# Expert gate and up columns in two slices of 1792 instead of four, with six PSUM banks taken in turn

## The chip, the cores and the metric

The kernel runs on one core of a Trainium2 chip. The metric is the time of one execution on the device in microseconds (us); the rows and the profile come from one execution taken by the hardware profiler, the other times from runs of the same program without it.

## What is computed

A two-layer encoder trunk on 256 tokens of 1024 features, all in float32: an attention mixer and a dense feed-forward in layer 0, an attention mixer and a mixture of experts in layer 1. The change touches the experts alone. There are eight, each with 3584 hidden columns, and each token goes to the two that its router ranks first:

```python
def swiglu(x, w_gate, w_up, w_down):
    return (jax.nn.silu(x @ w_gate) * (x @ w_up)) @ w_down
...
    for e in range(N_EXPERTS):
        y = y + combine[:, e:e + 1] * swiglu(xt, w_gate[e], w_up[e], w_down[e])
```

The kernel computes an expert only for the tokens sent to it, but it must read all three weight matrices: 3 x 1024 x 3584 x 4 bytes = 44.04 MB an expert, 352 MB for eight.

## The kernel before, in words

**Tokens in slots.** For a pair of experts, `gather` (L848) multiplies the tokens by a selection matrix, so that `gx` holds 128 token slots for each expert, features on the partitions. An expert uses 64 or 96 of them, in sets of 32: two sets for the three experts with few tokens ("narrow": the third, fifth and eighth to be computed), three for the other five ("wide"; `WIDE`). A set of 32 slots fills 32 columns of the TensorE array, so each matmul is written as four side by side (`q` in `gate_up`), each with a quarter of the weight columns; their outputs stand on four groups of 32 partitions.

**Slices.** `SLICES` (L886) cuts the 3584 columns into 1024, 1024, 768 and 768. For each slice `gate_up` (L914) runs through the gate matrix and then the up matrix. `load_raw` (L195) brings two chunks of 128 rows in one DMA: on each partition two runs of 4 KB (3 KB for the narrow slices), so four DMAs for each matrix and slice. For each chunk, set and `q` there is one matmul of 256 (192) columns (L929), recorded in the trace as two, with a weight load for each. Sets 0 and 1 of a matrix share a PSUM bank and the third sets of gate and up share another, so a slice takes two banks, or three if wide, from `mm_bank` (four, by turns). ACT then takes Silu of gate (L933, L938), DVE multiplies by up (L934, L939), and `h_turn` (L943) transposes the result on DVE in blocks of 32 into `hT`, which has two buffers. `down` (L957) multiplies `hT` by the slice's rows of the down matrix, 256 rows (1 MB, one run of 8 KB on each partition) a DMA, and adds all slices of an expert up in the banks a0 and a1.

**Order on TensorE.** The loop from L1068 issues the down product one slice late: gate and up of slice j, then the down product of slice j-1 (`late`), with the gather for the next pair between its steps at an odd expert's last slice. In slice 1 the previous expert's output is scattered: `scatter` (L990), once before `late` and once after it, two banks a2 and a3 each time, evicted by DVE (L1001); then `expert_start` (L900) transposes this expert's selection matrix in one bank. At the very end the last slice's down product follows the one before it directly, and then come the last scatter, the layer norm and the stores.

**Order on the DMA queue.** All weights are loaded by SP's queue in the order of their use. `raw_tile` (L152) takes the buffer from `rooms` (L1037), a fixed round of 20 buffers of 1 MB in various pools:

```python
    rooms += ([(extra[0], "xraw", {})] * 7 + [(wp, "raw", {})] * 4 + [(wp, "hi4", {"bufs": 1}), (wp, "lo4", {"bufs": 1})]
              + [(wp, "hi", {"bufs": 3}), (wp, "lo", {"bufs": 3})] * 3 + [(xp, "xTl", {})])
```

So a load starts when TensorE is done with the load 20 places before it, and SP waits at its head for that. The first 20 are issued while layer 1's mixer and router still run.

**Small tiles.** `pack` (L893, the slot numbers that `expert_start` compares with) lies in the buffer "gb" that the layer norms' scales used before; the experts' output `y` (L984) and `ST`, `hb`, `hT` lie in the pool `ep`.

Of the kernel before, what the change touches and what calls it, by code (L numbers as in the profile page):

```python
# [65 lines left out]
def tile_encoder(ctx: ExitStack, tc: tile.TileContext, x_in, emb_g, emb_b, w_in, b_gate, na_rpb, sw_sink,  # L66
# [13 lines left out]
    def mm_bank():  # L80
        return pp.tile([128, 512], F32, tag="mm", name="mm")
# [13 lines left out]
    def tr_bank():  # L95
        flip[0] ^= 1
        return acc_bank(2 + flip[0])
# [747 lines left out]
        dve.tensor_scalar(cmi, cmax, float(SLOTS), None, op0=OP.add)  # L845
        return res[0], res[1], who, cap, cmi

    def gather(S_sel, n, bank=lambda c2: mm_bank()):  # L848

        gx = xp.tile([128, KC, 256], F32, tag="xTh", name="gx")[:, :, :n]  # L850

        pss = {}

        def token_tile(c2, t):

            if not t:
                pss[c2] = bank(c2).rearrange("p (c s) -> p c s", c=2)[:, :, :n]
            for i in range(2):
                c = 2 * c2 + i
                for k, src in enumerate((xth, xtl)):  # L860
                    pe.matmul(pss[c2][:, i], src[:, t, c * 128:(c + 1) * 128], S_sel[:, t], start=i + k + t == 0,
                              stop=i + k + t == 3)

        def out(c2):
            g, b = ln_col(3, 2 * c2)
            act.activation(gx[:, 2 * c2], pss[c2][:, 0], AF.Identity, bias=b, scale=g)
            g, b = ln_col(3, 2 * c2 + 1)
            dve.tensor_scalar(gx[:, 2 * c2 + 1], pss[c2][:, 1], g, b, op0=OP.mult, op1=OP.add)

        def step(c2):  # L870
            for t in range(2):
                token_tile(c2, t)
            out(c2)

        return gx, [lambda c2=c2: step(c2) for c2 in range(KC // 2)], (token_tile, out)
# [7 lines left out]

    SLICES = [(0, 1024), (1024, 1024), (2048, 768), (2816, 768)]  # L886
    LASTJ = len(SLICES) - 1

    pack = {}

    def new_pack():

        pk = xp.tile([128, 256], F32, tag="gb", name="pack", bufs=1)  # L893
        pool.tensor_copy(pk[:, 0:128].rearrange("p (a s) -> p a s", a=2),
                         iota[:, None, 0:SA].to_broadcast([128, 2, SA]))
        pool.tensor_copy(pk[:, 128:256].rearrange("p (a s) -> p a s", a=4),
                         iota[:, None, SA:SLOTS].to_broadcast([128, 4, SB]))
        pack["rows"] = pk

    def expert_start(pcols, wide=True):  # L900

        S2 = part_tile([128, 2, 256], "S2")
        na = 1 + wide
        for t in range(2):
            dve.tensor_scalar(S2[:, t, 0:128 * na], pack["rows"][:, 0:128 * na], pcols(t), None, op0=OP.is_equal)
        ps = tr_bank().rearrange("p (a s) -> p a s", a=2)
        for a in range(na):
            for t in range(2):
                pe.transpose(ps[:, a, t * 128:(t + 1) * 128], S2[:, t, a * 128:(a + 1) * 128], ident)
        ST = ep.tile([128, 2, S], F32, name="ST")  # L910
        dve.tensor_copy(ST[:, 0:na], ps[:, 0:na])
        return ST

    def gate_up(wg, wu, gx, j, wide=True):  # L914

        c0, W = SLICES[j]
        nk, Q = 2048 // W, W // 4
        A, B = [], mm_bank() if wide else None
        for b, w in enumerate((wg, wu)):
            A.append(mm_bank())  # L920
            sets = [A[b][:, 0:Q], A[b][:, Q:2 * Q]] + ([B[:, b * 256:b * 256 + Q]] if wide else [])
            for kk in range(KC // nk):
                wt = load_raw(w[:, kk * nk:(kk + 1) * nk, c0:c0 + W], nk, W)
                for k in range(nk):
                    c = kk * nk + k
                    for s, out in enumerate(sets):

                        for q in range(4):
                            pe.matmul(out[q * 32:q * 32 + 32], gx[:, c, s * 32:s * 32 + 32],  # L929
                                      wt[:, k, q * Q:(q + 1) * Q], start=c == 0 and s != 1, stop=c == KC - 1 and s != 0)  # L930
        n = 3 if wide else 2
        h = part_tile([128, 512], "eh")[:, 0:2 * Q]
        act.activation(h, A[0][:, 0:2 * Q], AF.Silu)  # L933
        dve.tensor_mul(h, h, A[1][:, 0:2 * Q])  # L934
        parts = [(h, 2)]
        if wide:
            hb = ep.tile([128, 256], F32, name="hb")[:, 0:Q]
            act.activation(hb, B[:, 0:Q], AF.Silu)  # L938
            dve.tensor_mul(hb, hb, B[:, 256:256 + Q])  # L939
            parts.append((hb, 1))  # L940
        return parts

    def h_turn(parts):  # L943

        hT = ep.tile([128, 768], F32, name="hT", bufs=2)
        out = []
        at = 0
        for v, n in parts:
            N = v.shape[1]
            nb = N // n // 32  # L950
            dve.transpose(hT[:, at:at + N], v.rearrange("p (s f b) -> p s b f", s=n, f=32))
            out += [hT[:, at + i * 32 * nb:at + (i + 1) * 32 * nb].rearrange("p (b s) -> p b s", b=nb)
                    for i in range(n)]
            at += N
        return out

    def down(wd, hT, yb, j, between=(), final=False):  # L957

# [22 lines left out]
            step()  # L981

    def expert_out(yb):
        y = ep.tile([128, 2, 512], F32, name="y")  # L984
        act.activation(y[:, 0], yb[0], AF.Copy)
        if len(yb) > 1:
            dve.tensor_copy(y[:, 1], yb[1])
        return y[:, 0:len(yb)]

    def scatter(ST, y, ccols, t, bank=tr_bank):  # L990

        tk = slice(t * 128, (t + 1) * 128)
        pss = [bank() for _ in range(2)]
        k = y.shape[1]
        for a in range(k):
            for n in range(2):
                r = slice(n * 64, n * 64 + 64)
                pe.matmul(pss[n], ST[r, a, tk], y[r, a], start=a == 0, stop=a == k - 1)
        for n in range(2):
            ns = slice(n * 512, (n + 1) * 512)  # L1000
            dve.scalar_tensor_tensor(xt[:, t, ns], pss[n], ccols(t), xt[:, t, ns], op0=OP.mult, op1=OP.add)  # L1001
# [66 lines left out]
    for e in range(NE):  # L1068
        Sp, gx, _ = pair
        hs = slice(e % 2 * 128, e % 2 * 128 + 128)  # L1070
        wide = WIDE[e]
        if e < FIXED:
            wg, wu, wd = mgv[:, e], muv[:, e], moe_d[0, e:e + 1]
        else:
            it = nc.values_load(turns[2][0:1, e - FIXED:e - FIXED + 1], engines=[SP], min_val=0, max_val=NE - 1,
                                skip_runtime_bounds_check_because="a sum with one term, the index of an expert")
            wg, wu = (w[:, ds(it, 1)].rearrange("p e c n -> p (e c) n") for w in (mgv, muv))
            wd = moe_d[0, ds(it, 1)]
        for j in range(LASTJ + 1):
            final = e == NE - 1 and j == LASTJ  # L1080
            with ExitStack() as es:
                if e == j == 0:
                    es.enter_context(tc.manual_schedule(engines={PE}))
                h = gate_up(wg, wu, gx[:, :, hs], j, wide)
            hT = h_turn(h)
            if e == 0 and j == 1:
                comb = route_weights()
                turns += take_turns(comb)
            steps = []
            if j == LASTJ and e % 2 and e + 1 < NE:  # L1090
                pair = pair_start(e // 2 + 1)
                steps = pair[2]
            if j == 1 and ends:
                ends.pop(0)()
            if final:
                act.activation(sd[:, 0:1], eps, AF.Sqrt)
            if late:
                late(steps)
            if j == 1 and ends:
                ends.pop(0)()  # L1100
            if j == 1:
                ST = expert_start(lambda t: turns[0][:, t, e:e + 1], wide)
            if j == 0:
                yb = [acc_bank(n) for n in range(1 + wide)]

            def late(between, e=e, j=j, hT=hT, wd=wd, ST=ST if j else None, yb=yb, final=final):
                ccols = lambda t: turns[1][:, t, e:e + 1]
                down(wd, hT, yb, j, between, final)
                if j == LASTJ:
                    y = expert_out(yb)  # L1110
                    if not final:
                        ends.extend(lambda t=t: scatter(ST, y, ccols, t) for t in range(2))
                        return
                    for t in range(2):
                        scatter(ST, y, ccols, t, mm_bank)
                        out_part(t)
                        out_stats(t)

# [90 lines left out]
```

## Time and profile before

| | |
|---|---|
| runs | 1467.33, 1468.05, 1471.76 us (median 1468.05) |
| the profiled execution | 1467.57 us; its span on the core 1465.4 us |
| mean granted TensorE clock | 0.983 of 2.4 GHz |
| busy, share of the span | PE matmuls 95%, PE weight loads 71%, DVE 36%, ACT 23%, POOL 9% |
| instructions | 37823, of them 17251 matmuls and as many weight loads |
| DMA | 451.93 MB, 442.91 MB of it by SP's queue |

A matmul counts as busy from its start to a modelled end, and several run at a time, so a busy PE need not be at its limit. The DMA share is the busy time of the 16 DMA engines' packets; it can exceed 1, since packets of one engine overlap a little. Times in rows are microseconds from the start of the span. The experts' stage lasts from 595 us to the end.

### The profile page before, as it was taken

What the parts mean: (1) busy time and instruction counts of PE and PEld (TensorE: products, weight loads), DVE (VectorE), ACT (ScalarE), POOL (GpSimd) and SP (SyncE); (2) the same over time, 40 slices, a digit from 0 to 9 for tenths busy, and PEclk for the clock granted to TensorE, in tenths of its full rate; (3) what the DMA queues carried; (4) which work ended last, traced back from release to release, by engine and by line L of the source; (5) the groups of instructions that cost most, each with busy time, mean ns of one, the idle gap of its engine ahead of it and who ended that gap; (6) DMA issues with size and microseconds to landing.
All of it is one profiled execution on the core that took longest, in us unless ns stands there. A gap on an engine that the chain in (4) does not pass through costs nothing. (4 is left out here: it accounts for less than half of the span.)

```text
span 1465.4 us, 37823 instructions
## 1 busy us (share of the span) xinstructions
PE 1392.5 (95%) x17251; PEld 1033.5 (71%) x17251; DVE 521.5 (36%) x707; ACT 338.0 (23%) x543; POOL 125.6 (9%) x71
## 2 busy tenths in 40 slices
PE   7999989999899998899999999999979999999974
PEld 5989989999788896557967558766444475459741
DVE  8675685455687656501110210111201101210203
ACT  4566444444356752100000100001000000000000
POOL 5210050000360100400000000000000000000000
PEclk8999999999999999999999999999999999999998
DMA  8833546555483498699999999999999999999993
GB/s 293 236 126 128 173 132 230 184 173 173 144 238 118 123 395 302 211 343 411 408 335 403 409 407 410 408 408 410 408 408 411 396 404 410 401 400 411 399 409 148
DMA packets 155668, 451.93 MB, mean 308 GB/s; under 512 B 8032, under 2 KB 57568, under 8 KB 141296
## 3 DMA queue, kind: packets, MB, share of 16 engines
q1 hardware_dynamic: 153536, 442.91, 80.1%
q0 software_dynamic: 1968, 6.55, 1.5%
q8 instruction: 137, 2.24, 0.6%
q14 instruction: 27, 0.22, 0.0%
HBM read 448.38 MB, written 1.05 MB: 307 GB/s over the span
## 5 line engine op out<-in xcount | busy, mean ns | idle before, releaser
L929 PE MATMUL mm<-raw,gx 128*32 128x192 f32 (+1 forms) x10752 | 528.0, 353 | 15.9 <-DMA raw<-in_moe_w_up_dram 7.2
L929 PEld LDWEIGHTS mm<-raw,gx 128*32 128x32 f32 x10752 | 395.7, 110 | 149.7 <-issue 21.3
L971 PE MATMUL a<-raw,hT 128*32 128x512 f32 x1792 | 223.1, 600 | 14.4 <-DMA raw<-in_moe_w_down_dram 9.6
L934 DVE TENSOR_TENSOR eh<-eh,mm 128x512 f32<-128x512 f32 (+1 forms) x32 | 19.9, 621 | 583.6 <-PE mm L929 583.6
L192 DVE TENSOR_TENSOR lo<-raw,hi 128x2048 fp32r<-128x2048 f32 x78 | 191.6, 2464 | 89.9 <-ACT hi L185 89.7
L203 PE MATMUL mm<-xTh,hi 128*128 128x256 f32 x704 | 202.3, 287 | 0.0
L205 PE MATMUL mm<-xTh,lo 128*128 128x256 f32 x704 | 200.0, 284 | 0.0
L204 PE MATMUL mm<-xTl,hi 128*128 128x256 f32 x704 | 199.7, 284 | 0.0
L185 ACT ACTIVATE hi<-raw 128x2048 fp32r<-128x2048 f32 (+1 forms) x85 | 158.7, 1873 | 74.2 <-PE mm L204 43.2
L971 PEld LDWEIGHTS a<-raw,hT 128*32 128x32 f32 x1792 | 80.1, 111 | 120.3 <-issue 79.8
L203 PEld LDWEIGHTS mm<-xTh,hi 128*128 128x128 f32 x704 | 134.6, 191 | 7.2 <-issue 5.4
L205 PEld LDWEIGHTS mm<-xTh,lo 128*128 128x128 f32 x704 | 134.6, 191 | 3.1 <-issue 3.1
L204 PEld LDWEIGHTS mm<-xTl,hi 128*128 128x128 f32 x704 | 134.7, 191 | 1.8 <-issue 1.5
L933 ACT ACTIVATE eh<-mm 128x512 f32<-128x512 f32 (+1 forms) x32 | 17.4, 544 | 510.1 <-PE mm L929 510.1
L976 PE MATMUL a<-raw,hT 128*32 128x512 f32 x560 | 82.7, 592 | 0.0
L1124 POOL DMA_DIRECT2D raw<-in_ln_g_dram x1 | 0.6, 616 | 794.2 <-DMA raw<-in_moe_w_down_dram 794.2
L205 PE MATMUL mm<-hi,xTl 128*128 128x256 f32 (+1 forms) x128 | 46.6, 365 | 6.9 <-DVE xTl L273 6.9
L976 PEld LDWEIGHTS a<-raw,hT 128*32 128x32 f32 x560 | 28.7, 110 | 31.5 <-issue 27.8
L938 ACT ACTIVATE hb<-mm 128x256 f32<-128x256 f32 (+1 forms) x20 | 7.2, 358 | 186.0 <-PE mm L929 186.0
L203 PE MATMUL mm<-hi,xTh 128*128 128x256 f32 (+1 forms) x128 | 46.4, 367 | 3.8 <-DVE xTh L272 3.8
L204 PE MATMUL mm<-lo,xTh 128*128 128x256 f32 (+1 forms) x128 | 46.0, 361 | 0.2 <-DVE lo L192 0.2
L192 POOL TENSOR_TENSOR lo<-raw,hi 128x1024 fp32r<-128x1024 f32 (+1 forms) x7 | 23.9, 3416 | 249.4 <-ACT hi L185 249.4
(237 smaller groups left out, 1378.9 us busy)
## 6 DMA issues: line engine op xcount, KB each, us to landing
raw<-in_moe_w_down_dram SPq DMA_DIRECT2D x111, 1024.0 KB, 17.1
raw<-in_moe_w_gate_dram SPq DMA_DIRECT2D x64, 1024.0 KB, 18.6
raw<-in_moe_w_up_dram SPq DMA_DIRECT2D x64, 1024.0 KB, 18.3
raw<-in_moe_w_gate_dram SPq DMA_DIRECT2D x64, 768.0 KB, 17.7
raw<-in_moe_w_up_dram SPq DMA_DIRECT2D x64, 768.0 KB, 14.8
raw<-in_w_in_dram SPq DMA_DIRECT2D x32, 1024.0 KB, 6.2
raw<-in_ffn_w_gate_dram SPq DMA_DIRECT2D x11, 1024.0 KB, 5.5
raw<-in_ffn_w_up_dram SPq DMA_DIRECT2D x11, 1024.0 KB, 5.4
```

The lines of the kernel that those rows point to most:

```text
L185: act.activation(hi[:, p], raw[:, p], AF.Copy)
L192: eng.tensor_sub(lo[:, p], raw[:, p], hi[:, p])
L203: pe.matmul(o, lh, rh, start=first, stop=False)
L204: pe.matmul(o, lh, rl, start=False, stop=False)
L205: pe.matmul(o, ll, rh, start=False, stop=last)
L929: pe.matmul(out[q * 32:q * 32 + 32], gx[:, c, s * 32:s * 32 + 32], wt[:, k, q * Q:(q + 1) * Q], start=c == 0 and s != 1, stop=c == KC - 1 ...
L933: act.activation(h, A[0][:, 0:2 * Q], AF.Silu)
L934: dve.tensor_mul(h, h, A[1][:, 0:2 * Q])
L938: act.activation(hb, B[:, 0:Q], AF.Silu)
L971: pe.matmul(yb[0][r:r + 32], hT[s][:, m], w[:, n * 512:(n + 1) * 512], start=first, stop=last)
L976: pe.matmul(yb[1][r:r + 32], hT[2][:, m - 1 + i], wt[:, i, n * 512:(n + 1) * 512], start=j == 0 and m == 1, stop=last)
L1124: pool.dma_start(gf, ln2_g[1].partition_broadcast(128))
```

## The change

The columns are cut into two slices of 1792, one chunk of 128 rows a DMA (one run of 7 KB on each partition), eight DMAs for each matrix and slice; a buffer of 1 MB then holds 0.875 MB. A matmul has 448 columns. Each set of a matrix has a bank of its own, so a wide slice takes six and a narrow one four. All of them, and those of `scatter`, `gather` and `expert_start`, come from `late_bank`, which goes round the four `mm` banks and a2 and a3. `h` has one tile for all sets, in `ep`; `hT` has one buffer, so `h_turn` is moved behind `late`, and in the last slice it gets a buffer out of the weights' round instead. `pack` moves into `ep`, and `y` into "gb". With two slices the scatters, `expert_start` and the gather for the next pair all belong to slice 1.

```diff
-    SLICES = [(0, 1024), (1024, 1024), (2048, 768), (2816, 768)]
+    SLICES = [(0, FE // 2), (FE // 2, FE // 2)]
...
+    def late_bank():
+
+        spin[0] = (spin[0] + 1) % 6
+        return acc_bank(spin[0]) if spin[0] in (2, 3) else mm_bank()
...
-        pk = xp.tile([128, 256], F32, tag="gb", name="pack", bufs=1)
+        pk = ep.tile([128, 256], F32, name="pack")
...
-        ps = tr_bank().rearrange("p (a s) -> p a s", a=2)
+        ps = late_bank().rearrange("p (a s) -> p a s", a=2)
...
     def gate_up(wg, wu, gx, j, wide=True):
...
+        Q = W // 4
+        ns = 3 if wide else 2
+        banks = []
+        for w in (wg, wu):
+            outs = [late_bank()[:, 0:Q] for _ in range(ns)]
+            banks.append(outs)
+            for c in range(KC):
+                wt = load_raw(w[:, c:c + 1, c0:c0 + W], 1, W)[:, 0]
+                for s, out in enumerate(outs):
+                    for q in range(4):
+                        pe.matmul(out[q * 32:q * 32 + 32], gx[:, c, s * 32:s * 32 + 32], wt[:, q * Q:(q + 1) * Q],
+                                  start=c == 0, stop=c == KC - 1)
+        h = ep.tile([128, 3, FE // 8], F32, name="h")
+        for s in range(ns):
+            act.activation(h[:, s, 0:Q], banks[0][s], AF.Silu)
+            dve.tensor_mul(h[:, s, 0:Q], h[:, s, 0:Q], banks[1][s])
+        return h[:, 0:ns, 0:Q]
+
+    def h_turn(h, room=None):
+
+        ns, Q = h.shape[1:]
+        hT = (ep.tile([128, 3 * FE // 8], F32, name="hT") if room is None else room)[:, 0:ns * Q]
+        dve.transpose(hT, h.rearrange("p s (f b) -> p s b f", f=32))
+        return [hT[:, s * Q:(s + 1) * Q].rearrange("p (b s) -> p b s", s=32) for s in range(ns)]
...
     def expert_out(yb):
-        y = ep.tile([128, 2, 512], F32, name="y")
+        y = xp.tile([128, 2, 512], F32, tag="gb", name="y", bufs=1)
...
-        pss = [bank() for _ in range(2)]
+        pss = [late_bank() for _ in range(2)]
...
                 h = gate_up(wg, wu, gx[:, :, hs], j, wide)
-            hT = h_turn(h)
...
             if j == 0:
                 yb = [acc_bank(n) for n in range(1 + wide)]

+            hT = h_turn(h, raw_tile() if final else None)
+
             def late(between, e=e, j=j, hT=hT, wd=wd, ST=ST if j else None, yb=yb, final=final):
```

## Rows read from the trace of the kernel before

**Rows 1.** The page: GB/s in 40 equal slices of the span; costliest group of instructions

```profile
GB/s 293 236 126 128 173 132 230 184 173 173 144 238 118 123 395 302 211 343 411 408 335 403 409 407 410 408 408 410 408 408 411 396 404 410 401 400 411 399 409 148
...
L929 PE MATMUL mm<-raw,gx 128*32 128x192 f32 (+1 forms) x10752 | 528.0, 353 | 15.9 <-DMA raw<-in_moe_w_up_dram 7.2
```

**Rows 2.** Two stretches: length, busy time (count) by engine, clock, DMA share, GB/s

```profile
core 0: us, PE busy (x) PEld busy (x) DVE busy (x) ACT busy (x) POOL busy (x), PEclk, DMA share, GB/s
...
776.00:1395.00 619.00, 604.50 (x9716) 383.38 (x9717) 84.25 (x142) 27.90 (x55) 0.00 (x0) 0.99 1.02 407
...
598.00:776.00 178.00, 176.71 (x3021) 123.45 (x3009) 29.17 (x56) 6.66 (x14) 8.58 (x6) 1.00 0.97 362
```

**Rows 3.** SP's waits, 602 to 776 us: us in total, times, longest

```profile
SPq L199 <- PE mm L929: 100.3, 52, 4.5
```

**Rows 4.** SP's waits, 776 to 1395 us

```profile
SPq L199 <- DMA raw<-in_moe_w_up_dram: 113.4, 77, 2.2
```

**Rows 5.** PE's waits, 776 to 1446 us: us in total, times, longest

```profile
PE a L971 <- DMA raw<-in_moe_w_down_dram: 9.6, 10, 1.9
PE mm L929 <- DMA raw<-in_moe_w_up_dram: 7.2, 13, 2.0
PE a L971 <- SPq L1130: 4.8, 5, 2.6
...
PE mm L929 <- DMA raw<-in_moe_w_gate_dram: 3.2, 7, 0.7
```

**Rows 6.** Timeline of PE: start, length, what, count [idle before, and what ended it]

```profile
1074.79 1.92 PE L971 MATMUL a<-raw,hT 128*32 128x512 f32 x16 [1.00 <-DMA raw<-in_moe_w_down_dram]
...
1082.27 1.92 PE L971 MATMUL a<-raw,hT 128*32 128x512 f32 x16 [0.56 <-DMA raw<-in_moe_w_down_dram]
...
1086.19 1.51 PE L929 MATMUL mm<-raw,gx 128*32 128x192 f32 x32 [0.37 <-DMA raw<-in_moe_w_gate_dram]
...
1095.95 1.51 PE L929 MATMUL mm<-raw,gx 128*32 128x192 f32 x32 [0.46 <-DMA raw<-in_moe_w_up_dram]
1099.46 1.58 PE L929 MATMUL mm<-raw,gx 128*32 128x192 f32 x32 [2.00 <-DMA raw<-in_moe_w_up_dram]
...
1403.36 1.92 PE L971 MATMUL a<-raw,hT 128*32 128x512 f32 x16 [1.00 <-DMA raw<-in_moe_w_down_dram]
...
1443.05 3.64 PE L971 MATMUL a<-raw,hT 128*32 128x512 f32 x32 [0.47 <-SPq L1130]
```

**Rows 7.** DMA packets, 840 to 852 us; by queue: packets, MB, share of 16 engines

```profile
DMA packets 1525, 4.86 MB, mean 405 GB/s; under 512 B 90, under 2 KB 90, under 8 KB 1441
...
q1 hardware_dynamic: 1523, 4.82, 102.5%
```

**Rows 8.** DMA packets, 808 to 825 us

```profile
DMA packets 1765, 6.95 MB, mean 409 GB/s; under 512 B 107, under 2 KB 107, under 8 KB 1729
...
q1 hardware_dynamic: 1764, 6.93, 102.2%
```

**Rows 9.** DMA packets, 855 to 862 us

```profile
DMA packets 517, 2.86 MB, mean 408 GB/s; under 512 B 47, under 2 KB 47, under 8 KB 243
...
q1 hardware_dynamic: 516, 2.84, 99.4%
```

**Rows 10.** The instruction queue's packets, 776 to 1395 us

```profile
q8 instruction: 76, 1.25, 0.8%
```

**Rows 11.** The instruction queue's packets, 1075 to 1403 us

```profile
q8 instruction: 39, 0.64, 0.8%
```

**Rows 12.** GB/s in 40 equal slices of 511 to 598 us

```profile
GB/s 148 412 418 416 407 411 411 405 396 392 409 392 422 392 392 360 405 185 0 23 296 348 380 367 405 162 282 409 301 397 412 443 422 347 79 4 0 72 177 0
```

**Rows 13.** Line 929 alone in two stretches: length, PE and PEld busy (count), clock, DMA

```profile
597.00:635.00 38.00, 38.00 (x712) 21.13 (x708) 1.00 0.89 310
1319.00:1334.00 15.00, 14.56 (x361) 13.73 (x356) 1.00 1.02 409
```

**Rows 14.** Groups by shape, 600 to 1465 us: count, busy us, mean ns, idle before

```profile
L951 DVE STREAM_TRANSPOSE hT<-eh 128x512 f32<-128x512 f32 x16 | 17.9, 1122 | 0.6
...
L934 DVE TENSOR_TENSOR eh<-eh,mm 128x512 f32<-128x512 f32 x16 | 11.0, 688 | 287.6 <-PE mm L929 287.6
```

More of the change, by code (lines that the diff above doesn't have):

```diff
@@ L846, in take_turns, with gather @@
         return res[0], res[1], who, cap, cmi
-    def gather(S_sel, n, bank=lambda c2: mm_bank()):
+    def gather(S_sel, n, bank=lambda c2: late_bank()):
         gx = xp.tile([128, KC, 256], F32, tag="xTh", name="gx")[:, :, :n]
@@ L880, in select @@
             dve.tensor_scalar(S_sel[:, t, sl], iota, pcols(t), None, op0=OP.is_equal)
-    SLICES = [(0, 1024), (1024, 1024), (2048, 768), (2816, 768)]
+    SLICES = [(0, FE // 2), (FE // 2, FE // 2)]
     LASTJ = len(SLICES) - 1
     pack = {}
+    spin = [0]
+    def late_bank():
+        spin[0] = (spin[0] + 1) % 6
+        return acc_bank(spin[0]) if spin[0] in (2, 3) else mm_bank()
     def new_pack():
-        pk = xp.tile([128, 256], F32, tag="gb", name="pack", bufs=1)
+        pk = ep.tile([128, 256], F32, name="pack")
         pool.tensor_copy(pk[:, 0:128].rearrange("p (a s) -> p a s", a=2),
@@ L916, in gate_up @@
         c0, W = SLICES[j]
[L917 to L955, printed above, removed]
+        Q = W // 4
@@ L988, in expert_out, with scatter @@
         return y[:, 0:len(yb)]
-    def scatter(ST, y, ccols, t, bank=tr_bank):
+    def scatter(ST, y, ccols, t):
         tk = slice(t * 128, (t + 1) * 128)
-        pss = [bank() for _ in range(2)]
+        pss = [late_bank() for _ in range(2)]
         k = y.shape[1]
@@ L1114, in late @@
                     for t in range(2):
-                        scatter(ST, y, ccols, t, mm_bank)
+                        scatter(ST, y, ccols, t)
                         out_part(t)
```

## The prediction

> **What bounds the kernel now.** The page's GB/s by slices comes first [rows 1]: from the 19th slice on, about 660 us, the core moves some 400 GB/s with one dip, and it does so to the end. That is the experts' stage, which must read 352 MB. The windows then tell two parts of it apart [rows 2]: 362 GB/s at a DMA share of 0.97 from 598 to 776 us, and 407 GB/s at 1.02 from 776 to 1395 us. PE is busy throughout in both, but that count is no proof, so the waits decide.
>
> In the first part SP waits for TensorE alone, 52 times for matmuls of line 929 [rows 3]: the 20 buffers are full, and a load starts when a matmul gives one back. Two wide experts are computed there, and PE sets the pace. In the second part SP waits for landed loads too [rows 4], and PE stands waiting for loads, 9.6 + 7.2 + 4.8 + 3.2 = 24.8 us in all [rows 5]. (The 4.8 us are put down to SP's line 1130, but they lie in the last down product, whose steps come at the pitch of its loads; I count them as loads.) The timeline shows that pace: matmuls start 1.95 us apart on loads of 768 KB and 2.49 us apart on those of 1 MB [rows 6]. Wide experts put PE behind, narrow ones let it catch up, and the DMA engines never rest. So from 776 us to the last down steps, which run from 1443.05 to 1446.7 us, the DMA engines set the end; what follows, 18.7 us of a span of 1465.4, is untouched by the change.
>
> **The price of a run.** Three windows hold packets of mostly one size. In [rows 7] 90 packets are tiny, 1351 are of 3 KB and 82 of 8 KB; in [rows 8] 1622 are of 4 KB and 35 of 8 KB; in [rows 9] 196 are of 3 KB and 273 of 8 KB. Share x 16 engines x length gives 196.8, 278.0 and 111.3 us of packet time, from which follow 126.5 ns for 3 KB, 164.6 for 4 KB and 317 for 8 KB. A straight line through the latter two has 12 ns that do not depend on the size, and puts 7 KB at 278.9 ns. Shares above 1 mean that packets overlap a little, so these 12 ns are an upper bound.
>
> The pace of landing gives the net price. Each engine takes 16 packets of a 768 KB load: 5 loads from 1086.19 to 1095.95 us [rows 6], 1.952 us each, 122.0 ns a packet. A down load is 8 packets of 8 KB: 7.48 us for three, 2.493 each, 311.6 ns a packet. Their line has a fixed part of 8.2 ns and gives 159.9 ns for 4 KB (a 1 MB load of gate or up: 2.558 us) and 273.7 ns for 7 KB (a new load of 8 packets an engine: 2.189 us).
>
> **The change, part by part.**
>
> *Longer runs.* Two old loads take 2.558 + 1.952 us, two new ones 2 x 2.189: 0.066 us saved for each of 32 loads an expert. The number of loads stays 46 an expert, as do the bytes. The saving counts where DMA sets the pace, for the last six experts: 192 x 0.066 = **12.6 us**. No row has a packet of 7 KB. Upper bound, by the packets' own times: 8 x 12.2 ns x 192 = 18.7 us (25 us if all eight experts count). Lower bound, at 3 KB's rate by the byte: 1.952 x 7/6 = 2.277 us, a loss of 4 us. At 4 KB's rate by the byte, 2.238 us, 3 us are saved. I take the line, since packets on both sides of 7 KB lie on it.
>
> There is a rule against this. The Trainium skill, "DMA: Bandwidth & Descriptors", section "Bandwidth", puts the fixed overhead at about 3 cycles a packet beside one cycle for 32 bytes, and calls joining descriptors worth it only up to 256 bytes. By that page two runs of 3 and 4 KB become one for 227 instead of 230 cycles, an estimate of 1.3%, 5.6 us of the 433 us that those 192 loads take, and the sum below would end at 1455.3 us. The trace does not agree: its rows have more than twice that price a packet.
>
> *Fewer instructions to load.* Half as many matmuls for gate and up, each twice as wide on average. Wide experts have 1536 recorded matmuls there and narrow ones 1024 (5 and 3 of them make the 10752 of [rows 1]); three of each follow 776 us, so 3840 matmuls and 3840 weight loads go. The instruction queue fetched 76 packets of 16 KB while PE ran 9716 + 9717 instructions [rows 2, 10], 256 for each; 30 packets go. One packet takes 0.8% x 16 x 619 / 76 = 1.04 us on its engine, which delays everyone's landing somewhat: in [rows 6] one load comes 3.51 us after the one before it instead of 1.95. From 1074.79 to 1403.36 us lie exactly three experts' loads; at the pace above they need 3 x (16 x 2.558 + 16 x 1.952 + 14 x 2.493) = 321.2 us and took 328.6, with 39 such packets [rows 11]: 0.19 us each. **5.7 us** saved; if they spread evenly over the engines, 30 x 1.04 / 16 = 2 us.
>
> *The first two experts.* PE sets their pace. A matmul of 256 columns comes every 38/712 = 53.4 ns, one of 192 every 41.6 [rows 13]. At 256's rate by the column one of 448 takes 93.5 ns, and 24 of them 2.24 us a wide load; before, 48 took (2.56 + 2.00) / 2 = 2.28. Over 64 loads that saves 2.6 us, and by the line through both sizes 10 us; some evictions are added, so I take **1 us**, between nothing and 10. The 20 buffers, full from about 586 us while PE is not ready [rows 12], hold some 2.5 MB less then, 6 us of transfer. I take nothing: PE's release of buffers paces the loads from there to 776 us, its lead is 20 loads either way, and a load averages 44.04/46 MB before and after.
>
> *Banks and evictions.* As many elements are evicted, by DVE and ACT that are mostly idle. Six banks in one fixed round let the next gate phase start on banks that the last Silu freed half a slice ago, and scatter, gather and the selection's transposes take the following ones. Cover: gate's or up's eight loads, at least 12 us, beside three products of at most 0.69 us [rows 14]. If the cover is gone, see the second rival.
>
> *One hT, turned later.* The transposes of a slice now wait for the down product before it, and the next Silu, behind them on DVE's order, for them. 1344 columns at 1122/512 ns are 2.9 us [rows 14], while PE runs a gate phase. In the last slice, where no gate phase follows, the round's buffer lets them run beside seven loads of down, 17 us. Taken as nothing; uncovered, 16 x 2.9 = 47 us.
>
> *The rest.* SP issues as many loads in the same order and gets no new wait; the last hT takes one buffer of 20 for 14 loads while only 7 or so are under way. `pack` and `y` change places with neither read sooner than before. The gather's four steps move from among three down loads to among seven, so their evictions end earlier relative to the next gate phase. Nothing for each, an estimate of 1 us either way together.
>
> **Sum.** 12.6 + 5.7 + 1 = 19.3 us off the profiled execution's 1467.57: 1448.3 us. That execution stood 0.5 us under the median of the runs; I give **1448.5 us**. PE's 24.8 us of waiting [rows 5] shrink to a few; they are enough to let DMA's gain through, but not for much more than that.
>
> **Rivals.**
>
> *The runs were long enough.* The engine's time goes by the byte from 3 KB on, or 7 KB is cut into pieces again, so that the change does not do what it says to the queue. For it: 405, 409 and 408 GB/s in [rows 7 to 9] differ by 1%. Against it: the landing pitches, and 8 KB packets that go whole. Between a loss of 4 and a gain of 3 us by the bounds, with 2 to 5.7 us from the fetches: 1459 to 1470, middle 1464 us. The same page of the Trainium skill, section "Specifications", speaks for this rival: line rate from 512 bytes.
>
> *TensorE becomes the bound, at the turn of the banks.* A wide slice holds all six banks. If the scatter or the next gate phase had to wait for that slice's three Silus and three products, PE would stand up to 6 x 0.60 = 3.6 us (0.688 us at 448 of 512 columns; Silu taken as long) at each of 10 wide slices, 36 us against the 24.8 us that it has to spare: 11 us slower, 1479 us. It decides from 2.5 us a slice. Against it: the round is six, so the bank taken next was always read half a slice earlier; for it: PE already lags in wide experts, and scatter and transposes had a2 and a3 to themselves before.
>
> *Partly given back.* PE's spare time is used up by smaller stalls, of 1 us at each of 16 slices: 1455 to 1461 us.
>
> **Chances.** Forecast (1440 to 1455) 0.64; partly given back 0.14; runs long enough 0.14; TensorE the bound 0.08. The range, 1440 to 1464 us, reaches from the bounds' upper gain (18.7 + 5.7 + 3) to the middle of the first rival. A difference of 0.3%, 4.4 us, is what can be told from none: faster 0.64 + 0.14 + about 0.04 = 0.82, the same 0.10, slower 0.08.
>
> **What would show it.** Right: no 3 or 4 KB packets in the stage, and windows whose 7 KB packets take 275 to 280 ns; 30 instruction packets fewer from the third expert on; PE's waits for loads still there after 1050 us, though shorter. Wrong: SP waiting for PE alone after 776 us, PE's waits for ACT or DVE at slices' ends, or a landing pitch near 2.24 us for the new loads.

## The result and the profile after

| | before | after |
|---|---|---|
| median (runs) | 1467.36 us (1465.34 to 1471.76, 6 runs) | 1443.41 us (1441.67 to 1444.10, 6 runs) |
| the profiled execution | 1467.57 us, span 1465.4 | 1444.10 us, span 1442.2 |
| instructions | 37823 | 26993 |

The ratio is 0.9835 (95% interval 0.9823 to 0.9847), so 24 us were gained. The forecast was 1448.5, a gain of 19.3 us, and 1443.4 lies inside its range.

The page of after, GB/s in 40 equal slices; the instruction queue's packets; the costliest group [rows 1]:

```profile
GB/s 288 238 117 153 154 125 245 179 190 166 142 202 180 104 339 253 207 419 419 418 405 364 366 419 418 419 419 417 419 419 419 419 419 417 420 419 418 418 420 145
...
q8 instruction: 95, 1.56, 0.4%
...
L933 PE MATMUL mm<-raw,gx 128*32 128x448 f32 x3648 | 370.4, 540 | 1.9 <-DMA raw<-in_moe_w_up_dram 1.3
```

Where before stood between 396 and 411, after stands flat at 417 to 420, from the 24th slice to the last but one.

After's two stretches, by the columns of [rows 2]:

```profile
598.00:776.00 178.00, 178.00 (x1848) 57.68 (x1840) 22.32 (x41) 7.13 (x13) 6.82 (x3) 1.00 0.99 405
776.00:1372.00 596.00, 589.52 (x5728) 199.22 (x5724) 78.09 (x108) 26.69 (x48) 0.00 (x0) 1.00 1.01 412
776.00:820.00 44.00, 44.00 (x396) 16.42 (x396) 10.11 (x18) 3.35 (x6) 0.00 (x0) 1.00 0.89 330
820.00:860.00 40.00, 40.00 (x408) 13.13 (x404) 3.56 (x4) 1.69 (x3) 0.00 (x0) 1.00 1.01 419
```

The first stretch's rate rose the most, from 362 to 405 GB/s, though there TensorE was thought to set the pace. The last two rows split the second stretch: after's part paced by TensorE lasts not to 776 but to 820 us, for up to there the engines move only 330 GB/s, at a share of 0.89. SP's waits, 776 to 820 us, are for PE alone, which the prediction had named a sign of being wrong:

```profile
SPq L199 <- PE a L967: 21.9, 7, 4.1
SPq L199 <- PE mm L933: 12.3, 9, 3.7
SPq L199 <- PE a L933: 1.9, 2, 0.9
```

From 820 us on they are mostly for landed loads, and the rate is 419 GB/s.

After's DMA packets from 1200 to 1210 us, where nearly all are of 7 KB:

```profile
DMA packets 658, 4.21 MB, mean 421 GB/s; under 512 B 71, under 2 KB 71, under 8 KB 658
...
q1 hardware_dynamic: 658, 4.21, 101.7%
```

658 - 71 = 587 packets of 7 KB take 1.017 x 16 x 10 = 162.7 us, 277 ns each; the forecast said 278.9. The instruction queue's packets from 776 to 1380 us, about as far into the work as 1395 us is in before:

```profile
q8 instruction: 46, 0.75, 0.5%
```

That is 30 fewer than the 76 of [rows 10], as counted ahead. PE's waits of after, 776 to 1425 us:

```profile
PE a L962 <- DMA raw<-in_moe_w_down_dram: 12.4, 18, 2.0
PE a L962 <- SPq L1122: 2.3, 4, 0.6
PE mm L933 <- DMA raw<-in_moe_w_up_dram: 1.3, 2, 1.0
PE mm L989 <- ACT y L976: 0.8, 1, 0.8
PE a L989 <- ACT h L937: 0.7, 1, 0.7
PE mm L933 <- DMA raw<-in_moe_w_gate_dram: 0.6, 2, 0.4
```

The 24.8 us of waits for loads [rows 5] are 16.6 (12.4 + 2.3 + 1.3 + 0.6). The turn of the banks shows once: at 1051.78 us a scatter waits 0.7 us for a bank that Silu (L937) still reads. The other wait for ACT is the last scatter's; none for `hT` stands in the list. After's timeline of PE shows the pace:

```profile
1392.24 1.92 PE L962 MATMUL a<-raw,hT 128*32 128x512 f32 x16 [1.36 <-DMA raw<-in_moe_w_down_dram]
1394.73 1.93 PE L962 MATMUL a<-raw,hT 128*32 128x512 f32 x16 [0.56 <-DMA raw<-in_moe_w_down_dram]
...
1404.66 1.92 PE L962 MATMUL a<-raw,hT 128*32 128x512 f32 x16 [0.57 <-DMA raw<-in_moe_w_down_dram]
1407.23 1.92 PE L962 MATMUL a<-raw 128*32 128x512 f32 x16 [0.65 <-DMA raw<-in_moe_w_down_dram]
...
1419.57 3.64 PE L962 MATMUL a<-raw 128*32 128x512 f32 x32 [0.55 <-SPq L1122]
```

Down steps come (1404.66 - 1392.24) / 5 = 2.484 us apart, as before (2.493), and with the last of them the DMA engines are done: they still set the end.

**Where the time came from** is best read in bytes. The table gives what SP's queue moved in three stretches of each profiled execution; the kernels below after are told in the next section. Until 590 us it had moved 110.49 MB in before and 107.87 MB in all others (the 20 full buffers hold 2.62 MB less). The fourth column is POOL's queue. It brings the last layer norm's scale and bias, 1.05 MB, over the same 16 engines; after has moved most of that by 1390 us, before none. After's line of that queue from 860 to 1390 us, and before's from 1390 us on:

```profile
q0 software_dynamic: 252, 0.97, 0.5%
```

```profile
q0 software_dynamic: 288, 1.05, 3.5%
```

So the two queues are added up from 860 us on. Where DMA paces it, after moves (220.17 + 0.97) / 530 = 0.4173 MB a us.

| kernel | SP's MB, 590 to 860 us | SP's MB, 860 to 1390 us | POOL's MB, 860 to 1390 us | SP's MB left at 1390 us | its time, us |
|---|---|---|---|---|---|
| before | 98.29 | 214.05 | 0 | 20.09 | 1467.57 |
| after | 103.02 | 220.17 | 0.97 | 11.85 | 1444.10 |
| after, run again with half_runs | 103.32 | 220.07 | 1.04 | 11.66 | 1443.88 |
| after, run again with half_late | 103.29 | 220.06 | 1.04 | 11.69 | 1442.51 |
| half_runs | 101.81 | 215.97 | 0 | 17.26 | 1459.11 |
| narrow_mm | 102.29 | 219.21 | 0.36 | 13.54 | 1450.49 |
| both | 101.10 | 214.32 | 0 | 19.63 | 1465.50 |
| 18_buffers | 99.03 | 221.23 | 0 | 14.78 | 1451.16 |
| more_pe_early | 99.37 | 221.13 | 0 | 14.54 | 1452.60 |
| more_pe_late | 102.95 | 221.12 | 0 | 10.98 | 1443.84 |
| narrow_late | 100.21 | 219.65 | 0 | 15.18 | 1455.81 |
| narrow_early | 102.33 | 220.35 | 0.76 | 12.36 | 1445.36 |
| half_late | 102.95 | 216.13 | 0 | 15.96 | 1456.09 |
| late_norm | 104.91 | 220.10 | 1.05 | 10.04 | 1438.78 |

At 860 us after is 103.02 + 107.87 - 98.29 - 110.49 = 2.11 MB ahead, 5.1 us. From 860 to 1390 us it moves 221.14 - 214.05 = 7.09 MB more, 17.0 us. At 1390 us before has 21.14 MB of both queues left and after 11.93, a lead of 9.21 MB or 22.1 us. The remaining 1.4 us of the 23.5 between the two executions are about what before loses by taking its last 21.14 MB at its own pace (214.05 / 530 = 0.4039 MB a us: 52.3 us, against 50.7 at after's). POOL's 0.97 MB are 2.3 us of the lead.

### The profile page after: what moved, and what is told of

It is laid out like the page before. It is cut to its first block, busy times and chain, and to the rows that moved or that the text cites. A ratio compares the mean times of both kernels' runs of the same rounds, so it can differ in the third digit from the quotient of the medians.

```text
span 1442.2 us, 26993 instructions
## 1 busy us (share of the span) xinstructions
PE 1383.3 (96%) x11875; PEld 777.2 (54%) x11875; DVE 513.5 (36%) x661; ACT 336.3 (23%) x533; POOL 125.5 (9%) x71
## 3 DMA queue, kind: packets, MB, share of 16 engines
HBM read 448.38 MB, written 1.05 MB: 312 GB/s over the span
## 5 line engine op out<-in xcount | busy, mean ns | idle before, releaser
L933 PE MATMUL mm<-raw,gx 128*32 128x448 f32 x3648 | 370.4, 540 | 1.9 <-DMA raw<-in_moe_w_up_dram 1.3
L933 PEld LDWEIGHTS mm<-raw,gx 128*32 128x32 f32 x3648 | 117.1, 110 | 226.0 <-issue 209.6
L962 PE MATMUL a<-raw,hT 128*32 128x512 f32 x1680 | 197.5, 594 | 11.3 <-DMA raw<-in_moe_w_down_dram 11.3
L933 PE MATMUL a<-raw,gx 128*32 128x448 f32 x1728 | 187.4, 540 | 0.0
L938 DVE TENSOR_TENSOR h<-h,mm 128x448 f32<-128x448 f32 x32 | 19.9, 621 | 304.6 <-PE mm L933 302.0
L962 PEld LDWEIGHTS a<-raw,hT 128*32 128x32 f32 x1680 | 50.8, 110 | 135.4 <-issue 102.6
L933 PEld LDWEIGHTS a<-raw,gx 128*32 128x32 f32 x1728 | 55.4, 110 | 107.6 <-issue 102.9
L937 ACT ACTIVATE h<-mm 128x448 f32<-128x448 f32 x25 | 13.6, 544 | 320.1 <-PE mm L933 320.1
L967 PE MATMUL a<-raw,hT 128*32 128x512 f32 x560 | 72.8, 592 | 0.0
L945 DVE STREAM_TRANSPOSE hT<-h 128x1344 f32<-128x1344 f32 (+1 forms) x15 | 33.6, 2239 | 105.5 <-PE a L967 54.0
L976 ACT ACTIVATE y<-a 128x512 f32<-128x512 f32 x8 | 4.8, 597 | 270.9 <-PE a L962 270.9
## 6 DMA issues: line engine op xcount, KB each, us to landing
raw<-in_moe_w_gate_dram SPq DMA_DIRECT2D x128, 896.0 KB, 17.8
```

The source lines that it names most:

```text
L937: act.activation(h[:, s, 0:Q], banks[0][s], AF.Silu)
L938: dve.tensor_mul(h[:, s, 0:Q], h[:, s, 0:Q], banks[1][s])
L945: dve.transpose(hT, h.rearrange("p s (f b) -> p s b f", f=32))
L962: pe.matmul(yb[0][r:r + 32], hT[s][:, m], w[:, n * 512:(n + 1) * 512], start=first, stop=last)
L967: pe.matmul(yb[1][r:r + 32], hT[2][:, m - 1 + i], wt[:, i, n * 512:(n + 1) * 512], start=j == 0 and m == 1, stop=last)
```

## The experiments

Each kernel is the changed kernel with one edit; "above after" is the difference of medians against the changed kernel run again beside it. 18_buffers, the two more_pe kernels and late_norm had no such run beside them, so they are set against the first repeat's 1444.35 us, and a difference of a us or two says little there. The runs of before had medians of 1466.35, 1465.84, 1465.87 and 1467.37 us beside the four groups.

**The changed kernel again**, without an edit:

> The changed kernel again, as the yardstick of the runs beside it. Both theories expect 1443 us, 24 us under the kernel before (ratio 0.9835).

Measured: 1444.35 us (1443.88 to 1449.06, 4 runs), ratio 0.9862 [0.9845, 0.9878].

**Half runs:** each load of gate and up arrives as two runs of 3.5 KB a partition; matmuls and bytes as they were.

```diff
-                wt = load_raw(w[:, c:c + 1, c0:c0 + W], 1, W)[:, 0]
+                raw = raw_tile(only_extra[0]).rearrange("p (a b) -> p a b", a=2)[:, :, 0:W // 2]
+                nc.sync.dma_start(raw, w[:, c, c0:c0 + W].rearrange("p (a b) -> p a b", a=2))
...
```

> The changed kernel with only the runs of gate and up halved: each load stays one DMA of 896 KB, but its 7 KB on a partition go to two places 512 bytes apart, so that it is cut into packets of 3.5 KB. Instructions of TensorE, loads and buffers stay as they are. Theory (8.2 ns a packet, paid where the DMA engines set the pace): loads land 2.19 + 0.066 = 2.25 us apart, 12 us slower than the changed kernel (11 to 17), 1455 us. Rival (the runs were long enough and the gain came from elsewhere): within 3 us of the changed kernel, 1443 us.

Measured: 1456.15 us (1455.37 to 1459.11, 5 runs), ratio 0.9932 [0.9919, 0.9945], 11.8 us above after. Its SP queue from 860 to 1390 us:

```profile
q1 hardware_dynamic: 52772, 215.97, 101.8%
```

and that of after:

```profile
q1 hardware_dynamic: 33119, 220.17, 100.5%
```

4.20 MB less, though the engines were busier than in after. With the 0.97 MB of POOL's queue, which after moved there and half_runs did not, it is 5.17 MB, 12.4 us lost to the shorter packets alone, in that stretch.

**Narrow matmuls:** every gate and up matmul of 448 columns as two of 224; the loads as in after.

```diff
-                        pe.matmul(out[q * 32:q * 32 + 32], gx[:, c, s * 32:s * 32 + 32], wt[:, q * Q:(q + 1) * Q],
...
+                        for i in range(2):
+                            cs = slice(i * Q // 2, (i + 1) * Q // 2)
+                            pe.matmul(out[q * 32:q * 32 + 32, cs], gx[:, c, s * 32:s * 32 + 32],
+                                      wt[:, q * Q:(q + 1) * Q][:, cs], start=c == i == 0, stop=c == KC - 1 and i == 1)
```

> The changed kernel with each matmul of 448 columns of gate and up written as two of 224, so that TensorE runs as many instructions as before the change; the DMAs stay as they are. Theory (each instruction packet costs all loads about 0.19 us on average): 30 such packets more from the third expert on, 6 us slower than the changed kernel, 1449 us, and the long steps between landings come every 65 us instead of every 105. Rival (instruction packets are hidden): within 2 us, 1444 us.

Measured: 1450.33 us (1449.72 to 1460.1, 6 runs), ratio 0.9904 [0.9882, 0.9926], 6.0 us above after. Its queues from 860 to 1390 us:

```profile
q1 hardware_dynamic: 32982, 219.21, 100.4%
q8 instruction: 66, 1.08, 0.8%
```

26 instruction packets more than after's 40, and, with 0.36 MB on POOL's queue, 219.57 MB in all: 1.57 MB less than after, 3.8 us.

**Both** edits together.

> Both edits together: packets of 3.5 KB and matmuls of 224 columns, in two slices with the changed kernel's banks and order. Theory: the two costs add up, 18 us slower than the changed kernel, 1461 us, and 6 us under the kernel before is left for the first two experts and the stage's start. Rival (the slices' number and the banks bring most of the gain): under 1450 us.

Measured: 1464.0 us (1462.12 to 1467.91, 11 runs), ratio 0.9988 [0.9979, 0.9996], 19.7 us above after. All but 2.4 us of the gain over before (1466.35) is gone: longer packets and fewer instructions are nearly the whole of it. In 860 to 1390 us it moves 1.65 MB less than half_runs, 4.0 us, with 65 instruction packets against 39.

**18 buffers** instead of 20 in the round, to see whether the smaller load in each buffer costs lead.

```diff
+    rooms[5:7] = []
```

> The changed kernel with 18 buffers in the weights' round instead of 20. Theory (TensorE sets the pace in the first two experts, and what counts at their end is how many bytes the DMA engines are ahead, the round's length): two buffers fewer are 1.75 to 2 MB less ahead, 2.5 us each, 5 us slower than the changed kernel, 1448 us. Rival (only the steady rate of the DMA engines counts): within 1 us, 1443 us.

Measured: 1446.42 us (1443.24 to 1451.16, 4 runs), ratio 0.9858 [0.9839, 0.9877]. The interval overlaps that of after, so this does not show the cost that was expected. Nor does the edit quite do what its name says: the two entries leave the round, but their pool keeps seven buffers, and the first 20 loads still go ahead (107.87 MB until 590 us, as in after). Only later loads find the shorter round. Its profiled execution was the longest of the four, and its waits of PE (585 to 640 us) give one reason:

```profile
PE a L933 <- DVE gx L868: 3.5, 1, 3.5
```

Gate matmuls waited for the last `gx` eviction; after's profile has no such row (its second repeat has one of 0.9 us). This mishap comes back below.

**More TensorE work**, in the first two experts or in the last six: the first chunk's gate matmuls are done twice.

```diff
+                twice = more and c == 0 and w is wg
+                for rep in range(1 + twice):
...
+                                      start=c == 0, stop=c == KC - 1 or rep < twice)
...
-                h = gate_up(wg, wu, gx[:, :, hs], j, wide)
+                h = gate_up(wg, wu, gx[:, :, hs], j, wide, e < 2)
```

(`e >= 2` in the second kernel.)

> The changed kernel with the gate matmuls of the first chunk of each slice done twice (the second time overwrites the first) in the first two experts: 4 slices of 24 matmuls more, 2.25 us each, 9 us of TensorE. Theory (TensorE sets the pace there): all of it shows, 9 us slower than the changed kernel, 1452 us. Rival (the DMA engines set the pace all through): under 2 us, 1444 us.

> The same doubling in the last six experts instead: 6 wide slices of 2.25 us and 6 narrow ones of 1.5 us, 22.5 us of TensorE. Theory (the DMA engines set the pace there, and TensorE has 17 us or more to spare): 0 to 4 us slower than the changed kernel, 1443 to 1447 us. Rival (TensorE became the bound with the change): most of it shows, 15 us or more, over 1458 us.

Measured: early, 1452.6 us (1451.15 to 1453.97, 5 runs), ratio 0.9907 [0.9892, 0.9922], 8.3 us above after for 9 us of work. Late, 1446.85 us (1443.84 to 1453.08, 6 runs), ratio 0.9878 [0.9857, 0.9899], 2.5 us above after for 22.5 us of work. The late kernel's waits of PE, 600 to 1425 us, are two rows:

```profile
PE mm L991 <- ACT y L978: 0.8, 1, 0.8
PE a L964 <- SPq L1124: 0.5, 1, 0.5
```

So TensorE's time counts nearly in full in the first two experts, and in the last six it hides, more of it than the 16.6 us of after's waits: the late kernel's profiled execution, 1443.84 us, is no longer than after's 1444.10, and its engines move as much from 860 to 1390 us (221.12 MB against 221.14). Why its median is 2.5 us higher is not shown; the runs up to 1453.08 us have no profile.

The next group ran with the changed kernel once more:

> The changed kernel itself, run beside the three kernels below, so that each is compared on one chip: 1443 to 1446 us.

Measured: 1444.07 us (1442.51 to 1444.82, 4 runs), ratio 0.9853 [0.9839, 0.9868].

**Narrow matmuls in part of the experts:** the edit above under a condition, `e >= 2` (late) or `e < 2` (early).

> Gate and up matmuls of 224 columns instead of 448 for the last six experts alone; the loads are as in the changed kernel. Theory (instruction packets on the DMA engines delay the landing of weights by 0.19 us each, wherever DMA sets the pace): 30 more packets, 5.7 us more than the changed kernel, between 4 and 7. Rival (narrower matmuls cost the first two experts their pace on TensorE, and the packets hardly anything): at most 2 us more.

> Gate and up matmuls of 224 columns for the first two experts alone. There 3072 matmuls of 224 at 47.3 ns take the place of 1536 of 448 at 93.5: 1.8 us more of TensorE's time, and some 12 more instruction packets. Theory: 1.8 us more than the changed kernel, up to 4 if the packets count as well there. Rival (as above): 4 to 6 us more.

Measured: early, 1445.96 us (1445.36 to 1448.33, 4 runs), ratio 0.987 [0.9856, 0.9884], 1.9 us above after, as the theory said. Late, 1455.32 us (1446.75 to 1457.46, 6 runs), ratio 0.9919 [0.9899, 0.9939], 11.2 us above after: more than the same edit in all eight experts, against both theory and rival. The table tells why: 6.7 us of it (2.81 MB) are lost before 860 us, nearly all by 776 us (2.76 MB), where its matmuls are still those of after, and 3.6 us (1.49 MB of both queues) from 860 to 1390 us. Its waits of PE, 560 to 640 us:

```profile
PE a L936 <- DVE gx L868: 3.9, 1, 3.9
```

It is the row of 18_buffers again. DVE's timeline in narrow_late shows what held that eviction back:

```profile
593.19 1.11 DVE L868 TENSOR_SCALAR gx<-a,pcol 128x256 f32<-128x256 f32 x2
594.21 2.28 DVE L795 TENSOR_TENSOR v<-v,w 128x2 f32<-128x2 f32 x1
596.42 0.16 DVE L797 TENSOR_TENSOR comb<-oh,w 128x16 f32<-128x16 f32 x1
596.50 3.38 DVE L826 TENSOR_SCALAR turn<-turn_rk 128x6 f32<-128x6 f32 x4
599.80 0.53 DVE L868 TENSOR_SCALAR gx<-a,pcol 128x256 f32<-128x256 f32 x1
```

A product of 128x2 took 2.28 us, four small steps 3.38 us. POOL's timeline has two products of the layer norm just there:

```profile
594.12 4.66 POOL L237 TENSOR_TENSOR x<-x,gb 128x1024 f32<-128x1024 f32 x2 [3.85 <-DMA gb<-in_ln_b_dram]
```

POOL began 0.09 us ahead of DVE's product there. In after POOL began at 594.61, 0.37 us behind it, and the last `gx` eviction was done in time. Half a microsecond of POOL's start is what tells these two profiles apart. The wait is 3.9 of the 6.7 us. The rest is TensorE's clock: behind the wait the granted clock is 0.50, the 1.2 GHz level, from 600 to 606 us, and the gate matmul that starts at 599.44 us in after, where the clock is 1.00 by then, starts at 606.21:

```profile
600.00:606.00 6.00, 5.61 (x32) 1.55 (x36) 5.44 (x26) 0.00 (x0) 4.28 (x2) 0.50 0.44 151
```

(narrow_late's window, by the columns of [rows 2]).

**Half runs in the last six experts.**

> Two runs of 3.5 KB instead of one of 7 KB for the loads of gate and up of the last six experts alone. Theory (each packet has 8 ns that do not depend on its size, and what is lost counts where DMA sets the pace): nearly all of what halving them in all eight cost, 11.8 us, comes back: 9 to 12 us more than the changed kernel. Rival (the first two experts' loads count as much as the others): 6/8 of 11.8, 8.9 us or less.

Measured: 1458.25 us (1455.27 to 1466.07, 11 runs), ratio 0.9954 [0.9939, 0.9969], 14.2 us above after. That is over the theory's 9 to 12 and far from the rival's 8.9. In its profiled execution, 12.0 us above that of after, the first 860 us lose next to nothing (102.95 MB) and 860 to 1390 us lose 12.0 us (5.01 MB of both queues). Whether its runs up to 1466 us are late starts like narrow_late's is not shown; they have no profile. The longer runs' gain lies in the last six experts.

**Late norm:** POOL's layer norm waits for expert 0's first `h`, and so runs from 626 us on.

```diff
-    ln_apply(xt, bcast(ln1_g[1]), ln1_b[1], pool)
-    for t in range(2):
-        pool.tensor_scalar(xt[:, t], xt[:, t], ALPHA, None, op0=OP.mult)
...
+            if e == j == 0:
+                g = bcast(ln1_g[1])
+                dve.scalar_tensor_tensor(g[:, 0:1], h[:, 0, 0:1], 0.0, g[:, 0:1], op0=OP.mult, op1=OP.add)
+                ln_apply(xt, g, ln1_b[1], pool)
+                for t in range(2):
+                    pool.tensor_scalar(xt[:, t], xt[:, t], ALPHA, None, op0=OP.mult)
```

> The changed kernel with POOL's layer norm of layer 1 (lines 234, 237 and 1055) made to wait for the first h of expert 0, so that it runs about 30 us later; DVE's and TensorE's work is the same but for one small instruction. Theory (while POOL multiplies and adds there, single small instructions of DVE take 2 us and more instead of 0.2; two of them, 2.35 and 2.06 us, lie ahead of TensorE's 4.2 us wait for the slots, and in narrow_late others held the last gx back and cost 3.9 us): the wait shrinks to about nothing, the experts' stage starts 4 us earlier, and the time falls by 4 us, to 1438 to 1442; the runs also lie closer together. Rival (those instructions are slow for another reason, or the later layer norm and its transfer of 0.5 MB take as much from the experts' stage): 1443 to 1446.

Measured: 1437.58 us (1435.73 to 1438.78, 5 runs), ratio 0.9795 [0.9781, 0.9809], some 6 us below after and the fastest of all. That is just under the 1438 to 1442 that the theory gave. That the runs lie closer together is not shown: they span 3.1 us, after's 2.4, 5.2 and 2.3. After's DVE and PE, lines 787 and 861, and POOL's product:

```profile
585.03 4.64 POOL L234 TENSOR_TENSOR x<-x,gb 128x1024 f32<-128x1024 f32 x2 [1.23 <-DMA gb<-in_ln_g_dram]
...
585.06 2.35 DVE L787 TENSOR_TENSOR rt_tmp<-oh,lg 128x16 f32<-128x16 f32 x1
...
587.64 2.06 DVE L787 TENSOR_TENSOR rt_tmp<-oh,lg 128x16 f32<-128x16 f32 x1
...
590.24 0.55 PE L861 MATMUL a<-Sp,xth 128*128 128x256 f32 x1 [4.21 <-DVE turn_v L830]
```

The same instructions in late_norm:

```profile
585.75 0.18 DVE L787 TENSOR_TENSOR rt_tmp<-oh,lg 128x16 f32<-128x16 f32 x1
...
586.17 0.18 DVE L787 TENSOR_TENSOR rt_tmp<-oh,lg 128x16 f32<-128x16 f32 x1
...
586.88 0.36 PE L861 MATMUL a<-Sp,xth 128*128 128x256 f32 x1 [0.16 <-DVE turn_v L830]
...
626.10 4.74 POOL L234 TENSOR_TENSOR x<-x,gb 128x1024 f32<-128x1024 f32 x2 [41.61 <-DVE gb L1075]
```

The instructions take 0.18 us, PE's wait is 0.16 instead of 4.21, and the first gate matmul starts at 589.25 instead of 593.92 us, though POOL's transfer of the norm's bias now lies in the experts' stage.

## Why the prediction held, and which term was off

*What bounds the kernel.* Right in the main: the DMA engines set the end in both kernels, and most of the gain is theirs; more_pe_late shows it from TensorE's side. The border was drawn too sharply. In after TensorE sets the pace until 820 us, not 776. And SP waiting for PE alone, from which the prediction took TensorE's pace, does not prove it: in before the engines move 410 GB/s at a share of 1.02 from 660 to 740 us, in the midst of those waits (before's window, by the columns of [rows 2]):

```profile
660.00:740.00 80.00, 79.41 (x1352) 67.42 (x1355) 8.34 (x15) 3.33 (x7) 0.00 (x0) 1.00 1.02 410
```

*Longer runs, 12.6 us.* Right in its mechanism, and rather too small. In 860 to 1390 us the forecast's share is 12.6 x 220.17 / 264.2 = 10.5 us, and half_runs loses 12.4, half_late 12.0, so a packet's fixed part comes to some 9.4 to 9.7 ns instead of 8.2. By the medians the two lie 11.8 and 14.2 us above after. That rival, "the runs were long enough", is refuted. The page's rule of the Trainium skill, "DMA: Bandwidth & Descriptors", section "Bandwidth", gave 5.6 us, an estimate from its figures; these runs do not agree with it: they lost over twice as much.

*Fewer instructions to load, 5.7 us.* The count of 30 packets was right, the price of 0.19 us each too high. It was read from a stretch of before in which all else that delays a load was charged to them too. In 860 to 1390 us 26 packets cost 3.8 us (narrow_mm against after), 26 cost 4.0 (both against half_runs) and 27 cost 3.6 (narrow_late against after): 0.13 to 0.15 us each, which for 30 is 4.0 to 4.6 us. The runs' times agree: narrow_mm's 6.0 us less narrow_early's 1.9 leave 4.1 us.

*The first two experts, 1 us.* This is the term most off, though inside its "between nothing and 10". The lead at 860 us is 5.1 us, and 4.1 us of it (1.72 MB) were there at 820 us, where TensorE's pace ends, although 2.62 MB fewer had been loaded ahead. That smaller buffers cost nothing, as the prediction took, fits this, but 18_buffers does not test it cleanly. "A matmul of 448 columns takes 93.5 ns" was right, 428 of them in 40.00 us from 600 to 640. But I booked 1 of the 2.6 us that it saves, and more_pe_early and narrow_early show that TensorE's time counts nearly one to one there. Another part may come from ahead of the experts: the first gate matmul starts at 593.92 instead of 595.36 us. In other kernels here, late_norm aside, it lies between 592.32 (narrow_mm) and 595.44 (18_buffers), so up to 1.4 us of the gain may have nothing to do with the change; 2.6 and 1.4 are about the 4.1 us. What I did not see is that PE's and DMA's pace become nearly equal: 24 x 93.5 ns = 2.24 us beside 2.19 us for a load of 0.9175 MB at 419 GB/s. From 640 to 776 us PE is busy throughout and the engines run at their limit too:

```profile
640.00:776.00 136.00, 136.00 (x1400) 44.30 (x1392) 11.31 (x14) 5.50 (x10) 0.00 (x0) 1.00 1.01 415
```

(after's window, columns as above).

*The sum.* By the runs beside after: 11.8 (half_runs) + 6.0 (narrow_mm) are 17.8 of the 22.0 us of that group; both together 19.7; 2.4 us remain for everything else. The forecast's 12.6 + 5.7 + 1 = 19.3 is 4.7 us short of the 24.0 measured: by the bytes the first term was too small by about 2 us and the third by about 3, and the second too large by 1 to 2. That it came as near as it did is in part errors that cancel, which is luck.

*Banks, hT and evictions at nothing.* Right but for one wait of 0.7 us for a bank, which DMA's pace hides; "TensorE becomes the bound" wanted 2.5 us in each slice. "Partly given back" did not happen either: 16.6 us of PE's waits for loads were left, where the prediction had them shrink to a few and leave room for little more than DMA's gain. more_pe_late shows room for 22.5 us of TensorE's work. What is not settled is about 1 us of the 17.0 from 860 to 1390 us, which longer runs (12.0 to 12.4) and fewer instructions (25 packets, 3.3 to 3.8) leave over.

## What to carry to other kernels

Where DMA sets the pace, price runs by the pitch at which loads land at two sizes, and count the instruction queue's packets as DMA load too. Before booking a small or negative difference on an edit, compare the bytes moved up to a few fixed times, over all queues: they told the edit's cost from a late start that came ahead of the edit's work. SP's queue alone would have put the price of an instruction packet in narrow_late at 0.05 us, where both queues put it at 0.13. And look at single small instructions with long durations ahead of a stage's start; moving an elementwise job of POOL away from them was worth as much as a quarter of the whole change.

## What the runs showed of the hardware that was not expected

While POOL runs an elementwise product of 128x1024 (2.3 us each), a small DVE instruction that reads two tiles took 2.06 to 2.35 us instead of 0.18, and four small scalar steps 3.38 instead of 0.38; with POOL's work moved away all of them are short. In after each slow product ends as a product of POOL does: POOL's two run from 585.03 to 589.67 us, 2.32 us each, and DVE's end at 587.41 and 589.70. The Trainium skill, "SBUF — State Buffer", section "SBUF: two separate sides", has VectorE and GpSimd share one pair of ports that the first takes for its whole instruction; these rows agree with it.

TensorE's clock adds to it. In after the granted clock from 590.2 to 593.9 us, behind the 4.2 us in which PE stood, is 0.50, the 1.2 GHz level; 16 gather matmuls come 0.21 us apart:

```profile
590.20:593.90 3.70, 3.66 (x16) 3.49 (x16) 3.03 (x16) 2.96 (x5) 0.50 (x1) 0.50 0.39 148
```

In late_norm, where PE hardly stood, it is 1.00, the 2.4 GHz level, and they come 0.12 us apart:

```profile
586.80:589.20 2.40, 2.15 (x16) 1.97 (x16) 1.79 (x12) 1.95 (x4) 0.00 (x0) 1.00 0.04 10
```

So 1.3 of the 4.7 us by which the experts start earlier are the clock's.
